# The conditioning row's products on GpSimd and their sums on ScalarE, where one VectorE operation did both

## Chip, cores and metric

The kernel runs as one program on one core of a Trainium2 chip. The metric is the device time of one execution in microseconds (us), lower is better; the time before is 2505.53 us, the median of three runs (2505.07 to 2505.62).

## What is computed

Two transformer blocks over 256 tokens of 2048 features, all in float32. Block 1 has a gated delta rule, a block attention, a merge of both through an output projection, and a convolutional feed-forward layer. Block 2 has two layers, each with a sparse attention, a retention and an output projection; each layer is modulated by a conditioning row `c` (1 x 2048):

```python
c_act = jax.nn.silu(c)
for l in range(DEPTH_2):
    mod = c_act @ w_mod[l] + b_mod[l]            # 3 * 2048 outputs
    shift, scale, gate = jnp.split(mod, 3, axis=-1)
    h = rmsnorm(x, norm_gain[l]) * (1.0 + scale[:, None, :]) + shift[:, None, :]
    proj = h @ w_in[l]
    ...
    x = x + gate[:, None, :] * y
```

The change is about `c_act @ w_mod[l]` alone: a product of one row with a 2048 x 6144 matrix, per layer.

## The kernel before

**Large products.** Every weight matrix is cut into granules of 128 x 1024 numbers (some are narrower). `load_w` (line 208) loads one granule into a buffer `w` (four of them), has ScalarE round it to a high part `wh` (line 215, three buffers), and has VectorE subtract that from `w` to give a low part `wl` (line 216, four buffers). TensorE then makes three products per 128 x 128 tile: high by both parts of the tokens' tile, low by its high part. There are 867 granules. TensorE's order is the order of emission, written out in Python; the other engines' order is set by the tile scheduler, from the order of emission and its own idea of durations.

**The modulation as a background job.** `modulation` (line 987) is a generator. For each layer `l`, quarter `q` of the 2048 inputs and chunk `f` of 128 outputs it loads a tile `mw` of 128 outputs x 512 inputs (256 KB) and lets one VectorE operation multiply it by the conditioning row `mc` (copied to all partitions, after Silu) and sum along the row into one column; the operation starts from the column of the quarter before, so that sums go to and fro between `part` and `modT[l]`. That is 2 x 4 x 48 = 384 tiles. `mod_sums(3)` leaves the three newest loads for later, so that a load has time to land. There are four `mw` buffers (tag `sig`).

**Its pace.** `load_w` calls `pace` after every granule, and `pace` emits so many steps of each job per granule: for the modulation 0.75 in the mixers of block 1, 1.2 in the merge and the output projection of block 1, 0.35 in the feed-forward layer, 0.8 in block 2 (`RATE`, line 32). Where a pool of buffers ends, `mod_to` (line 1009) finishes what is loaded and moves on. `behind` (line 223) makes what a job emits come after the granule's load, cast and subtraction on their queues. So on VectorE's queue stand `wl` of a granule, then a product with the row; on SP's queue, which issues all loads in order, stand a `w`, then an `mw` that waits for its buffer, and behind it the next `w`.

**Where it is used.** Layer 0's modulation is needed by `gains(0)` (line 931) at the end of the feed-forward layer, layer 1's at the end of layer 0 of block 2.

**The places that the steps below touch.** The output projection of block 1 is the call of `outs` in `merge` (line 648); its `done` (line 643) adds the product to the residual stream `x` (line 644), sums squares (`acc`, line 358) and splits `x` into `v` (lines 318 and 319). The mixers' chains of small products are in `gdn` (line 695): TensorE, ScalarE (line 771) and VectorE (lines 746 and 782) take turns. GpSimd does nothing but the small powers of `pow` (line 328), 55 in all.

Of the kernel before, what the change touches and what calls it, by code (L numbers as in the profile page):

```python
# [14 lines left out]
P = 128  # L15
# [14 lines left out]
NRAW = 7                        # first chunks of block 1 on the tiles without 1/rms  # L30
PACE = 2.0                      # between the normalized tiles
RATE = (0.75, 1.2, 0.35, 0.8)   # modulation per granule: mixers, merge, ffn, block 2

# ---------------------------------------------------------------------------
# constants that depend on shapes alone


def _consts():
# [4 lines left out]
    cm = np.where(c <= u, 0.0, NEG).astype(f)          # [t, s]: key s may be read by query t  # L43
# [7 lines left out]
    mt = np.where(c >= u, 0.0, NEG)                     # [s, c]  # L51
# [21 lines left out]
    diff = c - u                                        # [s, t]: t - s  # L73
# [39 lines left out]
# ---------------------------------------------------------------------------  # L113
# [5 lines left out]
class Net:  # L119
    """The tensor engine runs in the order of emission. Chains of small products (the mixers' heads)  # L120
    are tasks: generators that yield the time until their next stage; their stages are emitted
    between the k tiles of the large products."""
# [26 lines left out]
    def finish(self, t):  # L149
        """emit what is left of a task (others go on in its waits)"""  # L150
        while not t.done:
            q = min(self.tasks, key=lambda u: (u.ready, u is not t))
            self.clk = max(self.clk, q.ready)
            self.step(q)

    def job(self, name, gen, rate):
        """small pieces of work, rate of them per granule of weights"""
        self.jobs[name] = [gen, rate, 0.0]
# [26 lines left out]
    # -- small helpers  # L185
# [22 lines left out]
    def load_w(self, src, n):  # L208
        """One granule of weights from DRAM, as hi + lo parts."""
# [12 lines left out]
    @contextlib.contextmanager  # L222
    def behind(self):
        """issue what follows after the latest granule"""
        with self.tc.issue_after(self.latest[0]), self.tc.issue_after(self.latest[1]), \
                self.tc.issue_after(self.latest[2]):
            yield

    def gemm_b(self, ps, grans, mov, start=True, stop=True, hold=False):
        """ps[f, t] += sum_k W[k, f] x[t, k]; grans: (dram ap [128, k * 128], k tile ids).  # L230
        hold: leave out the last k tile and return a function that emits it."""
# [16 lines left out]
    def outs(self, grans, mov, done, hold=2, mid=None):  # L248
        """chunks whose last k tile may be late: the first ones leave it out at first"""
# [15 lines left out]
    def chunk(self, w, mov):  # L265
        """w: dram ap [2, 128, 1024]"""
# [4 lines left out]
    def chunks3(self, w, mov):  # L271
        """three chunks, k tile by k tile (for moving tiles that are just being made); w: [8, 128, 768]"""
# [15 lines left out]
    def gemm_a(self, w, n, mov, prep=None):  # L288
        """two token tiles of x @ W[:, block]; w: dram ap [8, 128, 2n]"""
# [21 lines left out]
    def split(self, dst, src, scale=None, bias=None):  # L311
        """dst[:, 0] + dst[:, 1] = scale * src (+ bias), in two parts of 12 bits each."""
# [37 lines left out]
    # -- norms over the features of the residual stream  # L350
# [9 lines left out]
    def tok_sums(self, accs):  # L360
        """column sums of feature-major [128, T] tiles -> psum [128 tokens, 2 * len]"""
# [7 lines left out]
    def rows(self, col, n):  # L369
        """[128 tokens, n] columns (two per row) -> psum [128, n * 128] with each row on all partitions"""  # L370
# [21 lines left out]
    def side(self, which, width=T):  # L392
        """one of the two sets of 16 split [128, T] tiles"""
# [3 lines left out]
    def raw(self, dst, k, gcol, shift=None):  # L397
        """dst = x[k] times the gain, not yet normalized; with the shift as one more column"""
# [5 lines left out]
    def normalize(self, wait, accs, cols, hs, gcol, shift=None, out=None):  # L404
        """task: 1/rms of the residual stream, and its normalized, split tiles hs"""
# [17 lines left out]
    def trig(self, pool, pos, tabs, ptag):  # L423
        """cos and signed sin tables [128, T] of pos * inv; tabs: [128, 2] inverse frequency, sign"""
# [22 lines left out]
    def rotate(self, out, ps, cos, sin, half):  # L447
        """out = ps * cos + swap(ps) * sin on the first 2 * half partitions, a copy on the rest"""
# [12 lines left out]
    # ---------------------------------------------------------------------  # L461
# [26 lines left out]
    # ---------------------------------------------------------------------  # L488
# [15 lines left out]
    def mixers(self, bo, b1):  # L504
# [55 lines left out]
        def early():  # L560
            """a chunk on the tiles without 1/rms while the others are made"""
# [90 lines left out]
    def conv(self, dst, ps, tap, width, bias=None):  # L652
        """dst[:, t] = sum_j tap(j) * ps[:, t - (width - 1) + j] (+ bias)"""
# [9 lines left out]
    def gdn_gates(self, ps, r):  # L663
        """beta [128, h, tt], g [128, tt, h] and the decay exponents that go per key"""
# [30 lines left out]
    def gdn(self, h, kq, v, z):  # L695
# [6 lines left out]
        # per-token norms of k and q  # L702
# [11 lines left out]
        # decay between key s (partition) and query c: blocks (0,0), (0,1), (1,1)  # L714
# [11 lines left out]
        # S: K00 K01 Q00 Q01 K11 Q11, keys on partitions, scaled by beta / |k|^2  # L726
# [12 lines left out]
        # inverse of I + A per tile of 128 tokens, by doubling; DE[:, 0] the inverse, DE[:, 1] its transpose  # L739
# [17 lines left out]
        # values, tokens on partitions, times |k|  # L757
# [45 lines left out]
        # output norm; the query norm and 1/sqrt(128) go in as one factor per token  # L803
# [21 lines left out]
    def softmax_pv(self, pool, S, mx, scale, vcols, out):  # L825
        """S [128, 384]: logits of token tile 0 (128 keys), tile 1 (256 keys); mx [128, 2] their maxima.
        appends to out: pv [d, t] = sum_s v[s, d] softmax(scale * S)[t, s]"""
# [40 lines left out]
    # ---------------------------------------------------------------------  # L868
# [62 lines left out]
    def gains(self, l):  # L931
        """gains of the norms of block 2 with the modulation in them"""
# [9 lines left out]
    def bias_table(self, pool):  # L942
        """job: bias [128 t, 384] per head: tile 0 keys 0..127, tile 1 keys 0..255"""
# [12 lines left out]
        nr = pool.tile([P, 3 * P], F32, tag="leaf", name="nr", bufs=5)      # pos_s - pos_t  # L956
# [3 lines left out]
        bk = pool.tile([P, 3 * P], F32, tag="leaf", name="bk", bufs=5)      # bucket number  # L960
# [11 lines left out]
        def tree(h, l, i):  # L972
            """entry of the bucket among rows [i << (l + 1), (i + 1) << (l + 1)) of the table"""
# [13 lines left out]
    def modulation(self):  # L987
        """job: modT[l] [128, 48] = silu(c) @ w_mod[l] + b_mod[l], feature-major (shift, scale, gate)"""
        nc = self.nc
        part = self.per.tile([P, 48], F32, name="part")  # L990
        for l in range(2):
            for q in range(4):
                s = slice(q * 512, (q + 1) * 512)
                src, dst, pool = (part, self.modT[l], None) if q % 2 else (self.modT[l], part, None)
                for f in range(48):
# [7 lines left out]
                    self.mod_ahead.append((w, c, src[:, f:f + 1], dst[:, f:f + 1]))  # L1003
                    self.mod_sums(3)
                    yield
            self.mod_sums(0)
            self.mod_done = l + 1

    def mod_to(self, pool, rate):
        """go on with the modulation in another pool"""  # L1010
        self.mod_sums(0)
        self.pmo = pool
        self.jobs["mod"][1:] = [rate, 0.0]

    def mod_sums(self, left):
        while len(self.mod_ahead) > left:
            w, c, src, dst = self.mod_ahead.pop(0)
            self.nc.vector.tensor_tensor_reduce(w, w, c, 1.0, src, OP.mult, OP.add, dst)  # L1018

    # ---------------------------------------------------------------------  # L1020
# [11 lines left out]
    def prepare(self, row):  # L1032
        """job: the residual stream of block 2 itself, and tables of the retention"""
# [11 lines left out]
    def layer(self, l):  # L1045
# [50 lines left out]
        # keys of the attention, with both gains and 1/rms in them  # L1096
        ka = b2.tile([P, T], F32, tag="ka", name="ka", bufs=1)
        key = self.add(self.keys(l, nxt(), ka))
        # queries
# [293 lines left out]
```

## Time and profile before

| | |
|---|---|
| median of three runs | 2505.53 us (2505.07 to 2505.62) |
| span of the profiled execution | 2502.3 us, first to last instruction |
| TensorE busy | 2486.1 us, 99% of the span |
| VectorE busy | 1931.8 us, 77% |
| ScalarE busy | 1400.8 us, 56% |
| GpSimd busy | 44.9 us, 2% |
| granted TensorE clock | 1.000 of full speed (2.4 GHz) |

The profiled execution's own time is not given beside its span; the runs' median is 3.2 us above the span, which is what lies before the first instruction and after the last. In the rows below, PE is TensorE, PEld its weight loads, DVE VectorE, ACT ScalarE, POOL GpSimd and SP the queue that issues the loads. A row of a wait names who waited, who released it, and the time in all. A matmul's end is modelled, so a busy TensorE is not one at its peak.

### The profile page before, as it was taken

What the parts mean: (1) busy time and instruction counts of PE and PEld (TensorE: products, weight loads), DVE (VectorE), ACT (ScalarE), POOL (GpSimd) and SP (SyncE); (2) the same over time, 40 slices, a digit from 0 to 9 for tenths busy, and PEclk for the clock granted to TensorE, in tenths of its full rate; (3) what the DMA queues carried; (4) which work ended last, traced back from release to release, by engine and by line L of the source; (5) the groups of instructions that cost most, each with busy time, mean ns of one, the idle gap of its engine ahead of it and who ended that gap; (6) DMA issues with size and microseconds to landing.
All of it is one profiled execution on the core that took longest, in us unless ns stands there. A gap on an engine that the chain in (4) does not pass through costs nothing.

```text
span 2502.3 us, 51550 instructions
## 1 busy us (share of the span) xinstructions
PE 2486.1 (99%) x20410; PEld 2474.0 (99%) x20410; DVE 1931.8 (77%) x3737; ACT 1400.8 (56%) x2240; POOL 44.9 (2%) x59
## 2 busy tenths in 40 slices
PE   8999999999999999999999999999999999999999
PEld 8999999999999999999999999999999999999999
DVE  8777778577799989889876679897887677666664
ACT  7555556534455656777754456655844456475443
POOL 0000000000000000000000000000000000000000
PEclk9999999999999999999999999999999999999999
DMA  6444476588889667767666767668676554444554
GB/s 240 169 154 161 149 228 226 200 281 304 297 286 306 211 215 213 237 218 218 234 219 213 238 216 218 210 216 275 212 239 220 180 185 167 157 169 167 176 185 159
DMA packets 189012, 536.06 MB, mean 214 GB/s; under 512 B 21600, under 2 KB 26464, under 8 KB 188768
## 3 DMA queue, kind: packets, MB, share of 16 engines
q1 hardware_dynamic: 188768, 532.75, 64.1%
q8 instruction: 160, 2.62, 0.4%
q14 instruction: 84, 0.69, 0.1%
HBM read 530.57 MB, written 2.10 MB: 213 GB/s over the span
## 4 chain that ended last, share of the span: by engine, by line
PE 96%; DVE 2%; ACT 1%; issue 0%; POOL 0%; DMA 0%; SPq 0%; DVEq 0%; POOLq 0%
PE mm L179 89%; PE aux L179 6%; PE aux L183 1%; DVE wl L216 0%; DVE isc L1228 0%; DMA w<-wA 0%; DVE mw L1018 0%; ACT wh L215 0%; DVE m L1232 0%; DVE isc L1233 0%; POOL rq L328 0%; DVE acc L358 0%; ACT L724 0%; ACT v L318 0%; POOL gf L328 0%
## 5 line engine op out<-in xcount | busy, mean ns | idle before, releaser
L179 PE MATMUL mm<-u,wh 128*128 128x256 f32 (+1 forms) x7488 | 1366.8, 284 | 0.0
L215 ACT CAST wh<-w 128x1024 fp32r<-128x1024 f32 (+5 forms) x867 | 854.1, 986 | 906.9 <-PE mm L179 752.6
L216 DVE TENSOR_TENSOR wl<-w,wh 128x1024 fp32r<-128x1024 f32 (+5 forms) x867 | 990.8, 1144 | 393.2 <-ACT wh L215 389.1
L179 PEld LDWEIGHTS mm<-u,wh 128*128 128x128 f32 x7488 | 1150.1, 189 | 3.9 <-issue 2.9
L179 PE MATMUL mm<-u,wl 128*128 128x256 f32 (+1 forms) x3744 | 1052.1, 281 | 0.0
L179 PE MATMUL mm<-v,wh 128*128 128x256 f32 (+1 forms) x4096 | 742.6, 283 | 0.0
L179 PEld LDWEIGHTS mm<-u,wl 128*128 128x128 f32 x3744 | 705.3, 188 | 0.0
L179 PEld LDWEIGHTS mm<-v,wh 128*128 128x128 f32 x4096 | 629.1, 189 | 0.8 <-issue 0.5
L179 PE MATMUL mm<-v,wl 128*128 128x256 f32 (+1 forms) x2048 | 576.4, 281 | 2.2 <-DVE wl L216 2.2
L179 PEld LDWEIGHTS mm<-v,wl 128*128 128x128 f32 x2048 | 385.8, 188 | 3.4 <-DVE wl L216 3.3
L1018 DVE CUSTOM_DVE_ANT_0 mw<-mw,mc,part 128x512 f32<-128x512 f32 x192 | 141.6, 744 | 4.3 <-ACT mc L1000 3.2
L1018 DVE CUSTOM_DVE_ANT_0 mw<-mw,mc,mod 128x512 f32<-128x512 f32 x192 | 142.2, 745 | 2.6 <-ACT mc L1000 2.5
L179 PE MATMUL mm<-wh,u 128*128 128x412 f32 (+1 forms) x320 | 88.9, 346 | 0.0
L976 ACT ACTIVATE leaf<-bit,row,dr 128x384 f32<-128x384 f32 x120 | 78.8, 698 | 0.0
L660 DVE SCALAR_TENSOR_TENSOR u<-mm,par,u 128x255 f32<-128x255 f32 (+1 forms) x160 | 76.3, 477 | 2.8 <-ACT u L658 2.1
L179 PE MATMUL mm<-wh,v 128*128 128x412 f32 (+1 forms) x256 | 69.8, 350 | 5.6 <-ACT wh L215 5.6
L179 PE MATMUL mm<-more,wh 128*128 128x256 f32 x384 | 69.7, 281 | 0.0
L179 PEld LDWEIGHTS mm<-wh,u 128*128 128x128 f32 x320 | 59.0, 188 | 0.4 <-issue 0.2
L179 PEld LDWEIGHTS mm<-more,wh 128*128 128x128 f32 x384 | 59.0, 189 | 0.0
L980 DVE COPY_PREDICATED leaf<-bit,leaf 128x384 f32<-128x384 uint32 x88 | 53.3, 605 | 3.4 <-ACT leaf L976 2.8
L179 PEld LDWEIGHTS mm<-wh,v 128*128 128x128 f32 x256 | 48.2, 192 | 6.7 <-ACT wh L215 6.6
L179 PE MATMUL mm<-wl,u 128*128 128x412 f32 (+1 forms) x160 | 54.2, 338 | 0.0
(293 smaller groups left out, 2014.5 us busy)
## 6 DMA issues: line engine op xcount, KB each, us to landing
w<-wB SPq DMA_DIRECT2D x344, 512.0 KB, 3.8
mw<-wM SPq DMA_DIRECT2D x384, 256.0 KB, 3.8
w<-wUp SPq DMA_DIRECT2D x170, 512.0 KB, 4.1
w<-wO SPq DMA_DIRECT2D x96, 512.0 KB, 4.3
w<-wDn SPq DMA_DIRECT2D x64, 384.0 KB, 3.5
w<-wDn SPq DMA_DIRECT2D x64, 320.0 KB, 3.4
w<-wA SPq DMA_DIRECT2D x48, 412.0 KB, 3.2
w<-wBr SPq DMA_DIRECT2D x32, 512.0 KB, 4.2
```

Of the source, the lines that this page charges most:

```text
L179: self.nc.tensor.matmul(out, l, r, start=start, stop=stop)
L183: self.nc.tensor.transpose(out, in_, self.c0("ident"))
L215: i1 = nc.scalar.copy(h[:, :n], w[:, :n])
L216: i2 = nc.vector.tensor_tensor(l[:, :n], w[:, :n], h[:, :n].bitcast(F32), op=OP.subtract)
L660: nc.vector.scalar_tensor_tensor(dst[:, s:], ps[:, :T - s], tap(width - 1 - s), dst[:, s:], op0=OP.mult, op1=OP.add)
L976: nc.scalar.activation(t, bits[0], ACT.Identity, scale=dr[:, i, h:h + 1], bias=rb[:, i, 0, h:h + 1])
L980: nc.vector.copy_predicated(t, bits[l].bitcast(mybir.dt.uint32), u)
L1018: self.nc.vector.tensor_tensor_reduce(w, w, c, 1.0, src, OP.mult, OP.add, dst)
```

## The change

Each tile `mw` is multiplied by the row in place by GpSimd, and a copy in place by ScalarE sums it along the row into a column of its own (`accum_out`). The columns of the four quarters no longer pass through one another: `part` has one per layer, quarter and chunk, and four small VectorE additions per layer put them together with the bias. The product is emitted two loads after its own, the sum three loads after, where the one VectorE operation stood. The scratch for dynamic DMA descriptors is made smaller (1024), and comments are left out; nothing else differs.

```diff
     def modulation(self):
...
-        part = self.per.tile([P, 48], F32, name="part")
+        part = self.per.tile([P, 2, 4, 48], F32, name="part")
         for l in range(2):
             for q in range(4):
                 s = slice(q * 512, (q + 1) * 512)
-                src, dst, pool = (part, self.modT[l], None) if q % 2 else (self.modT[l], part, None)
+                pool = None
                 for f in range(48):
...
                     w = pool.tile([P, 512], F32, tag="sig", name="mw", bufs=4)
                     nc.sync.dma_start(w, self.a["wM"][l, q, f])
-                    self.mod_ahead.append((w, c, src[:, f:f + 1], dst[:, f:f + 1]))
-                    self.mod_sums(3)
+                    self.mod_ahead.append([w, c, part[:, l, q, f:f + 1]])
+                    self.mod_sums(2, 3)
                     yield
-            self.mod_sums(0)
+            self.mod_sums()
+            for q in range(4):
+                nc.vector.tensor_tensor(self.modT[l], self.modT[l], part[:, l, q], op=OP.add)
             self.mod_done = l + 1
...
-    def mod_sums(self, left):
+    def mod_sums(self, loading=0, left=0):
+        nc = self.nc
+        for m in self.mod_ahead[:max(0, len(self.mod_ahead) - loading)]:
+            if m[1] is not None:
+                nc.gpsimd.tensor_tensor(m[0], m[0], m[1], op=OP.mult)
+                m[1] = None
         while len(self.mod_ahead) > left:
-            w, c, src, dst = self.mod_ahead.pop(0)
-            self.nc.vector.tensor_tensor_reduce(w, w, c, 1.0, src, OP.mult, OP.add, dst)
+            w, _, col = self.mod_ahead.pop(0)
+            nc.scalar.activation(w, w, ACT.Copy, accum_out=col)
...
-    nc = bacc.Bacc("TRN2", target_bir_lowering=False, num_devices=1)
+    nc = bacc.Bacc("TRN2", target_bir_lowering=False, num_devices=1, dynamic_dma_scratch_size=1024)
```

In the changed code the product stands in line 1022, the sum in line 1026 and the additions in line 1008. TensorE's instructions and their order are the same in both.

VectorE's queue before, in the output projection of block 1 (`x` is the residual stream, `acc` the sum of squares, `v` its split; L1018 is the product with the row, whose second row, with one column, reads the sum out):

```order
L216 TENSOR_TENSOR wl<-w,wh 128x1024
L1018 ISA mw,mod<-mw,mc,part 128x512
L1018 ISA mod 128x1
L644 TENSOR_TENSOR x_72<-x_72,mm 128x256
L216 TENSOR_TENSOR wl<-w,wh 128x1024
L358 TENSOR_TENSOR acc<-acc,sq 128x256
L319 SCALAR_TENSOR_TENSOR v_9102<-x_72,par,v_9102 128x256
L1018 ISA mw,mod<-mw,mc,part 128x512
L1018 ISA mod 128x1
L216 TENSOR_TENSOR wl<-w,wh 128x1024
```

The same place now:

```order
L216 TENSOR_TENSOR wl<-w,wh 128x1024
L644 TENSOR_TENSOR x_72<-x_72,mm 128x256
L216 TENSOR_TENSOR wl<-w,wh 128x1024
L358 TENSOR_TENSOR acc<-acc,sq 128x256
L319 SCALAR_TENSOR_TENSOR v_9267<-x_72,par,v_9267 128x256
L216 TENSOR_TENSOR wl<-w,wh 128x1024 x2
```

The products are gone from VectorE's queue, and the subtractions stand closer together.

ScalarE's queue before, in the same projection, a few granules later:

```order
L215 CAST wh<-w 128x1024 x2
L357 ACTIVATE sq<-x_73 128x256
L318 ACTIVATE v_9106<-x_73,par 128x256
L215 CAST wh<-w 128x1024 x2
L357 ACTIVATE sq<-x_73 128x256
```

And now, at the end of layer 0's modulation (`part` takes the sums):

```order
L215 CAST wh<-w 128x1024
L357 ACTIVATE sq<-x_73 128x256
L318 ACTIVATE v_9272<-x_73,par 128x256
L1026 ACTIVATE mw,part<-mw 128x512
L215 CAST wh<-w 128x1024
L1026 ACTIVATE mw,part<-mw 128x512
L215 CAST wh<-w 128x1024
L357 ACTIVATE sq<-x_74 128x256
L318 ACTIVATE v_9273<-x_74,par 128x256
L1026 ACTIVATE mw,part<-mw 128x512 x4
L215 CAST wh<-w 128x1024
```

A sum, which waits for GpSimd's product, stands between the casts, and four in a row where the layer's last loads are finished.

GpSimd's queue now, from the mixers to the feed-forward layer (`gcp`, `gf` and `rc` are the powers of norms, which stood next to one another before):

```order
L328 TENSOR_TENSOR gcp<-gcs,cst_79 128x4
L1022 TENSOR_TENSOR mw<-mw,mc 128x512 x5
L328 TENSOR_TENSOR gf<-gso,cst_79 128x2
L1022 TENSOR_TENSOR mw<-mw,mc 128x512 x10
L328 TENSOR_TENSOR gf<-gso,cst_79 128x2
L1022 TENSOR_TENSOR mw<-mw,mc 128x512 x151
L328 TENSOR_TENSOR rc<-rc,cst_79 128x2
```

The powers now stand behind the products, one to ten of them apart in the mixers.

## Rows read from the trace of the kernel before

**Rows 1.** The page's busy time, share of the span and instructions of each engine.

```profile
PE 2486.1 (99%) x20410; PEld 2474.0 (99%) x20410; DVE 1931.8 (77%) x3737; ACT 1400.8 (56%) x2240; POOL 44.9 (2%) x59
```

**Rows 2.** TensorE's waits: who released it, us in total, times, longest.

```profile
PE mm L179 <- ACT wh L215: 5.6, 3, 4.6
PE mm L179 <- DVE wl L216: 3.7, 7, 1.1
PE aux L179 <- ACT gR L771: 2.6, 2, 2.0
```

**Rows 3.** Busy us by stretch: from:to and length, PE, PEld, DVE, ACT, POOL, clock, DMA.

```profile
0.00:100.00 100.00, 91.05 (x688) 87.07 (x689) 79.16 (x165) 73.16 (x134) 3.96 (x7) 1.00 0.63 218
100.00:200.00 100.00, 96.36 (x808) 94.51 (x808) 72.39 (x150) 51.10 (x105) 4.47 (x5) 1.00 0.46 154
```

**Rows 4.** The same for merge (first) and output projection of block 1 (second).

```profile
500.00:690.00 190.00, 190.00 (x1604) 190.00 (x1604) 147.78 (x259) 77.66 (x91) 0.00 (x0) 1.00 0.86 295
690.00:820.00 130.00, 130.00 (x1098) 130.00 (x1098) 117.84 (x235) 65.42 (x98) 0.00 (x0) 1.00 0.85 288
```

**Rows 5.** The same two stretches, VectorE's operations on the tile mw alone.

```profile
500.00:690.00 190.00, 57.82 (x79) 1.00 0.86 295
690.00:820.00 130.00, 40.10 (x55) 1.00 0.85 288
```

**Rows 6.** VectorE's groups by form: busy us, mean ns, idle before and its releaser.

```profile
L216 DVE TENSOR_TENSOR wl<-w,wh 128x1024 fp32r<-128x1024 f32 x642 | 784.8, 1223 | 319.9 <-ACT wh L215 317.6
L1018 DVE CUSTOM_DVE_ANT_0 mw<-mw,mc,mod 128x512 f32<-128x512 f32 x192 | 142.2, 745 | 2.6 <-ACT mc L1000 2.5
L1018 DVE CUSTOM_DVE_ANT_0 mw<-mw,mc,part 128x512 f32<-128x512 f32 x192 | 141.6, 744 | 4.3 <-ACT mc L1000 3.2 <-DMA mw<-wM 1.1
...
L216 DVE TENSOR_TENSOR wl<-w,wh 128x640 fp32r<-128x640 f32 x64 | 52.5, 820 | 16.7 <-ACT wh L215 16.5
```

**Rows 7.** ScalarE's groups by form, and the casts of the projection's stretch (last).

```profile
L1000 ACT ACTIVATE mc<-mc 128x512 f32<-128x512 f32 x11 | 6.9, 628 | 10.9 <-DMA mc<-c 10.9
...
L833 ACT ACTIVATION_READ_ACCUMULATOR aS<-aS,snm 128x1 f32 x32 | 6.0, 187 | 0.0
...
L215 ACT CAST wh<-w 128x1024 fp32r<-128x1024 f32 x43 | 45.1, 1050 | 53.3 <-PE mm L179 44.1 <-issue 7.0 <-ACT v L318 2.0
```

**Rows 8.** GpSimd's groups: busy us, mean ns, idle before.

```profile
L328 POOL TENSOR_TENSOR brs<-bve,cst 128x2 f32<-128x2 f32 x16 | 11.1, 696 | 474.2 <-DVE bve L1280 474.2
L328 POOL TENSOR_TENSOR gcp<-gcs,cst 128x4 f32<-128x4 f32 x8 | 8.2, 1027 | 125.6 <-DVE gcs L708 125.6
```

**Rows 9.** Timeline: start us, us, engine; a power alone, and one beside VectorE.

```profile
1653.98 0.69 POOL L328 TENSOR_TENSOR rq<-hr,cst 128x2 f32<-128x2 f32 x1 [5.16 <-DVE hr L1185]
...
1703.15 1.00 DVE L216 TENSOR_TENSOR wl<-w,wh 128x824 fp32r<-128x824 f32 x1
...
1703.31 1.40 POOL L328 TENSOR_TENSOR rq<-hr,cst 128x2 f32<-128x2 f32 x1 [3.94 <-DVE hr L1185]
```

**Rows 10.** VectorE's groups by form in the stretch 690 to 820 us.

```profile
L216 DVE TENSOR_TENSOR wl<-w,wh 128x1024 fp32r<-128x1024 f32 x43 | 52.4, 1220 | 10.0 <-ACT wh L215 9.8
...
L319 DVE SCALAR_TENSOR_TENSOR v<-x,par,v 128x256 fp32r<-128x256 f32 x16 | 7.6, 477 | 0.0
...
L358 DVE TENSOR_TENSOR acc<-acc,sq 128x256 f32<-128x256 f32 x15 | 6.3, 417 | 0.0
L319 DVE SCALAR_TENSOR_TENSOR u<-mrg,u 128x256 fp32r<-128x256 f32 x16 | 6.0, 416 | 0.0
...
L216 DVE TENSOR_TENSOR wl<-w,wh 128x768 fp32r<-128x768 f32 x3 | 2.8, 950 | 0.4 <-ACT wh L215 0.4
L634 DVE TENSOR_TENSOR mrg<-sig 128x256 f32<-128x256 f32 x5 | 2.1, 419 | 0.1
```

**Rows 11.** All waits: ScalarE's casts for a buffer that TensorE gives back.

```profile
ACT wh L215 <- PE mm L179: 752.6, 553, 4.2
```

**Rows 12.** The page's loads: times, KB each, median us from issue to landing.

```profile
mw<-wM SPq DMA_DIRECT2D x384, 256.0 KB, 3.8
```

More of the change, by code (lines that the diff above doesn't have):

```diff
@@ L1002, in modulation @@
                     nc.sync.dma_start(w, self.a["wM"][l, q, f])
-                    self.mod_ahead.append((w, c, src[:, f:f + 1], dst[:, f:f + 1]))
-                    self.mod_sums(3)
+                    self.mod_ahead.append([w, c, part[:, l, q, f:f + 1]])
+                    self.mod_sums(2, 3)
                     yield
-            self.mod_sums(0)
+            self.mod_sums()
+            for q in range(4):
+                nc.vector.tensor_tensor(self.modT[l], self.modT[l], part[:, l, q], op=OP.add)
             self.mod_done = l + 1
     def mod_to(self, pool, rate):
-        self.mod_sums(0)
+        self.mod_sums()
         self.pmo = pool
         self.jobs["mod"][1:] = [rate, 0.0]
-    def mod_sums(self, left):
+    def mod_sums(self, loading=0, left=0):
[4 more added lines that the diff above has]
+                m[1] = None
         while len(self.mod_ahead) > left:
-            w, c, src, dst = self.mod_ahead.pop(0)
-            self.nc.vector.tensor_tensor_reduce(w, w, c, 1.0, src, OP.mult, OP.add, dst)
+            w, _, col = self.mod_ahead.pop(0)
+            nc.scalar.activation(w, w, ACT.Copy, accum_out=col)
     def block2(self, b2):
```

## The prediction, made blind

> **What bounds the kernel now.** I read the busy times first, then TensorE's waits, then the busy time stretch by stretch. TensorE is busy for 2486.1 of 2502.3 us, 99%, and its instructions are the same after the change [rows 1]. So 16.2 us is all that the profile shows as idle, and the waits put it down to few places: the casts and subtractions of the first granules, and a chain in the mixers that waits for ScalarE's copy `gR`, 2.6 us in two waits [rows 2]. By stretch, 8.95 us of the idle time lie in the first 100 us and 3.64 us in the second [rows 3]; in the merge and in the output projection of block 1 TensorE never stops [rows 4]. VectorE (77%) and ScalarE (56%) run ahead of it: ScalarE's casts wait 752.6 us for a buffer that TensorE has to give back, in 553 waits [rows 11]. That is how a reader sees who sets the pace: the helper waits for the bound engine, not the other way.
>
> The job begins after the first heads, so of the idle time it could reach only the mixers' 3.6 us and scraps. A measurement of this kernel can tell about 0.2%, 5.0 us, from no change. More than that can't be gained, whatever VectorE is spared; the question is whether TensorE begins to wait.
>
> **The change, part by part.** The median of the runs, 2505.5 us, is 3.2 us above the span; I add my terms to the median, since nothing in the change touches what lies outside the span.
>
> *VectorE loses* 384 operations of 0.745 us, 283.8 us busy [rows 6], and gains eight additions of 48 columns. In the projection it is busy for 117.8 of 130 us [rows 4], of which the products are 40.1 [rows 5]. All of it is hidden under TensorE today: 0 us gained.
>
> *ScalarE gains* 384 copies of 128 x 512 with a sum. A Silu of that size takes 0.628 us and reading out a sum 0.187 us [rows 7]: at most 0.82 us each, 313 us in all, and ScalarE goes to about 1714 us, 68%. In the merge that makes 77.7 + 79 x 0.82 = 142 of 190 us, in the projection 65.4 + 55 x 0.82 = 110 of 130 us [rows 4, 5]. The cover is the casts' waiting for TensorE, 44.1 us of the projection [rows 7], and 45 us are wanted there: just enough, if no sum waits. Cost 0.
>
> *GpSimd gains* 384 products of 128 x 512, which no row shows. From below: VectorE's own pass, 0.745 us [rows 6]. From above: a power of two columns takes 0.696 us and one of four 1.027 [rows 8], 0.166 us per column, which for 512 columns would be 85 us a product and 33 ms in all. A power is another computation, and the row that the product is nearest to is a plain subtraction: from 640 to 1024 columns it grows from 820 to 1223 ns, 1.05 ns per column [rows 6]. I take GpSimd's 0.70 us of two columns as what every instruction costs and add 512 columns at that rate, 0.54 us: 1.23 us. If the two operands are read one after the other, it is 0.70 + 1.08 = 1.78 us, the upper end that I keep. GpSimd is then busy for some 517 us, 21%.
>
> For the same product the Trainium skill, GPSIMD Engine Reference, section "Performance versus the Vector engine", gives 4497 ns for 2048 columns, and calls it about twice VectorE's time; my estimate from that page for 512 columns is a quarter, 1.12 us, and the sum below would stand. No run here shows it.
>
> *The wait that is added.* A sum now waits for a product, and the product for its load; behind the sum on ScalarE's queue stand the next cast, and for that cast wait VectorE's subtraction and TensorE. The freed `mw` buffer lets SP issue the next load, and behind that stand the weights. Four buffers and 79 products in 190 us [rows 5] make a turn of 4 x 2.41 = 9.6 us. Landing 3.8 us [rows 12], product 1.23 and sum 0.82 make 5.9 us: 3.8 us are left, and with 1.78 us still 3.2. In the projection the turn is 4 x 2.36 = 9.5 us. Cost 0.
>
> *The five places where loads are finished at once* (three ends of pools, two ends of layers) leave no such room: the last sum follows its load at once, and what comes on top is one product, 1.23 us. The casts are one to two granules ahead (46 granules in 130 us are 2.8 us each [rows 4, 10]), so I let a quarter through: 5 x 0.3 = 1.5 us. From below 0, from above 5 x 1.78 = 9 us.
>
> *The mixers.* VectorE's share gets lighter, ScalarE's copies get a neighbour, and GpSimd's powers stand behind products. Between losing the 3.6 us of idle time and adding as much again I take 0.
>
> *GpSimd beside VectorE.* The timeline shows that GpSimd can be made to wait: a power that takes 0.69 us alone takes 1.40 us when it starts beside a subtraction, and ends 0.56 us after that subtraction does (1704.71 against 1704.15) [rows 9]. The other direction, VectorE waiting for a long GpSimd product, no row can show, since a power reads two columns. I bound it. If it never happens: 0. If every product stops VectorE for its whole 1.23 us: in the merge 79 x 1.23 = 97 us, against 42.2 us that VectorE is idle and 57.8 us that it is spared, 100 in all: it fits. In the projection 55 x 1.23 = 67.7 us, against 12.2 + 40.1 = 52.3 us: 15.4 us too much. But a product meets VectorE only when the next operation has two operands in SBUF, if it is as beside the subtraction, which has two [rows 9]. Those are the subtractions, `v`, `acc`, `u` and `mrg` [rows 10]: 52.4 + 2.8 + 7.6 + 6.3 + 6.0 + 2.1 = 77.2 of 130 us, 59%. 0.59 x 67.7 = 40 us, less than 52.3. I take 0, and keep 15.4.
>
> Sum: 2505.5 + 1.5 = **2507 us**.
>
> **The rivals.**
>
> *GpSimd's products hold up VectorE in the output projection of block 1* (the call in line 648). Then the subtractions come late, one after another, until TensorE has used up what is done ahead. The price is worked out above: 15.4 us, less one granule of 2.8 us that is ahead at its start, plus the 1.5: 2505.5 + 14 = 2520 us. It decides from 52.3 / 55 = 0.95 us that a product costs VectorE on average. For it speaks that GpSimd waits to the end of a subtraction, so something is shared [rows 9], and that VectorE has only 12.2 us to spare there [rows 4]. Against it speaks the 59%. Chance 0.25.
>
> The Trainium skill, SBUF — State Buffer, section "Who interferes with whom", states this as a rule against the change: a VectorE instruction with two SBUF inputs and a GpSimd instruction that reads SBUF share a read port, and whichever comes second is blocked until the first is done. The trace agrees with one half of it, 1.40 against 0.69 us [rows 9]; if both halves hold fully the time is this rival's.
>
> *Lateness on the short chains.* `gcp` and `gf` are sixteen powers in the mixers on which later stages wait, and each may find half a product before it: 16 x 0.62 = 10 us if nothing hid it. ScalarE's sums may delay the `gR` copies, whose two waits cost 1.3 us each today [rows 2]. TensorE has rows of large products between the stages, so I let two thirds through: 2505.5 + 6.6 = 2512 us. Chance 0.09.
>
> *A gain.* With VectorE lighter the mixers' idle 3.6 us [rows 3] go: 2505.5 - 3.6 = 2502 us. It would need more than all of it to be told from no change. Chance 0.03.
>
> That the change doesn't do what it says is no rival: the queues shown above have the products on GpSimd and the sums on ScalarE.
>
> **How the numbers follow.** The forecast has 0.63, the rivals 0.25, 0.09 and 0.03. Slower by over 5 us are the first two rivals: 0.34. Faster by over 5 us: 0.03. Within: 0.63. The range must leave out no more than 2 in 10: it goes down to 2503, short of the full gain, and up to 2520, the first rival's price; products of 1.78 us would cost more (55 x 1.78 = 98 us against 52.3), and with part of the gain are what I leave out. The forecast's own range is 2503 to 2510.
>
> **What would show it.** Right: TensorE busy again for some 2486 us, and its waits for `wl` and `wh` still a few us; VectorE at 1650 to 1750 us; ScalarE near 1700; GpSimd near 520, with products of 1.1 to 1.4 us; the casts still waiting for TensorE, less than 752.6 us. Wrong: subtractions of 128 x 1024 whose mean has grown well over 1.22 us, and TensorE idle between 690 and 820 us waiting for `wl` (first rival); waits of TensorE's small products on ScalarE or GpSimd between 100 and 470 us (second); products of 1.8 us or more, with ScalarE's sums waiting for GpSimd and casts late behind them.

## Result and the profile after

The changed kernel takes **2546.4 us** (median of four runs, 2543.99 to 2550.18) against 2505.6 us before, measured beside it: ratio 1.0164, 95% interval 1.015 to 1.0178. It is 41 us slower. The forecast was 2507 us, and the range ended at 2520.

First the page's busy times after the change, the answer to [rows 1]:

```profile
PE 2503.6 (98%) x20410; PEld 2483.2 (98%) x20410; DVE 1906.6 (75%) x2977; ACT 1628.3 (64%) x3008; POOL 650.5 (26%) x443
```

Two numbers were not foreseen. VectorE lost 283.8 us of products [rows 6] and is busy only 25.2 us less: what it has left takes 1906.6 - (1931.8 - 283.8) = 258.6 us longer, 0.67 us per product of GpSimd. And TensorE, with the same instructions, is idle for 2542.2 - 2503.6 = 38.6 us in place of 16.2, and "busy" for 17.5 us more.

TensorE's waits, the answer to [rows 2] (who waited, who released it, us in all, times, longest):

```profile
PE mm L179 <- DVE wl L216: 16.9, 24, 1.9
PE aux L179 <- ACT gR L771: 7.0, 4, 3.1
PE mm L179 <- ACT wh L215: 6.8, 4, 4.6
```

VectorE's low parts `wl` are late 24 times in place of 7, for 16.9 us in place of 3.7; the mixers' `gR` 4 times in place of 2. Next VectorE's groups by form, the answer to [rows 6] (busy us, mean ns of one, idle before and its releaser):

```profile
L216 DVE TENSOR_TENSOR wl<-w,wh 128x1024 fp32r<-128x1024 f32 x642 | 854.9, 1333 | 343.7 <-ACT wh L215 341.3 <-issue 0.3
...
L216 DVE TENSOR_TENSOR wl<-w,wh 128x640 fp32r<-128x640 f32 x64 | 58.7, 917 | 18.8 <-ACT wh L215 18.5
```

The same subtractions take 1333 ns in the mean in place of 1223, and 917 in place of 820. The output projection of block 1 now runs from 707 to 846 us. Its groups answer to [rows 10]:

```profile
L216 DVE TENSOR_TENSOR wl<-w,wh 128x1024 fp32r<-128x1024 f32 x43 | 72.4, 1686 | 9.8 <-ACT wh L215 9.7
L319 DVE SCALAR_TENSOR_TENSOR v<-x,par,v 128x256 fp32r<-128x256 f32 x15 | 15.5, 1032 | 0.0
L319 DVE SCALAR_TENSOR_TENSOR u<-mrg,u 128x256 fp32r<-128x256 f32 x16 | 13.8, 895 | 0.0
L358 DVE TENSOR_TENSOR acc<-acc,sq 128x256 f32<-128x256 f32 x14 | 13.5, 963 | 0.0
L644 DVE TENSOR_TENSOR x<-x,mm 128x256 f32<-128x256 f32 x16 | 6.5, 409 | 0.4 <-PE mm L179 0.4
```

Four groups have grown: `wl` from 1220 to 1686 ns, `v` from 477 to 1032, `u` from 416 to 895, `acc` from 417 to 963. The fifth has not: `x<-x,mm` reads one operand from PSUM (`mm` is TensorE's result), and takes 409 ns; it was 416. In this stretch all groups that have grown read two operands in SBUF. For comparison GpSimd's product, ScalarE's sum and its read-out, over the whole execution:

```profile
L1022 POOL TENSOR_TENSOR mw<-mw,mc 128x512 f32<-128x512 f32 x384 | 606.5, 1588 | 1173.9 <-DMA mw<-wM 849.3
```

```profile
L1026 ACT ACTIVATE mw<-mw 128x512 f32<-128x512 f32 x384 | 240.4, 626 | 16.7 <-POOL mw L1022 16.1
...
L1026 ACT ACTIVATION_READ_ACCUMULATOR mw<-mw 128x1 f32 x384 | 72.5, 189 | 0.0
```

The timeline shows single pieces (start us, us, engine). First VectorE, then GpSimd, in the projection, and then in the mixers:

```profile
770.40 0.41 DVE L644 TENSOR_TENSOR x<-x,mm 128x256 f32<-128x256 f32 x1
770.73 1.99 DVE L216 TENSOR_TENSOR wl<-w,wh 128x1024 fp32r<-128x1024 f32 x1
772.64 1.51 DVE L358 TENSOR_TENSOR acc<-acc,sq 128x256 f32<-128x256 f32 x1
774.08 1.52 DVE L319 SCALAR_TENSOR_TENSOR v<-x,par,v 128x256 fp32r<-128x256 f32 x1
775.52 1.21 DVE L216 TENSOR_TENSOR wl<-w,wh 128x1024 fp32r<-128x1024 f32 x1
```

```profile
765.67 9.64 POOL L1022 TENSOR_TENSOR mw<-mw,mc 128x512 f32<-128x512 f32 x5
```

```profile
226.97 1.23 DVE L813 SCALAR_TENSOR_TENSOR gf<-gf,gcp 128x2 f32<-128x2 f32 x1 [0.62 <-POOL gf L328]
```

```profile
226.91 1.28 POOL L1022 TENSOR_TENSOR mw<-mw,mc 128x512 f32<-128x512 f32 x1
```

While five products run one after another, from 765.67 to 775.31 us, every two-SBUF operation beside them is stretched; at 775.52, with GpSimd at rest, a subtraction takes 1.21 us again. In the mixers an operation of two columns starts 0.06 us after a product and lasts 1.23 us, until the product is over (226.91 + 1.28 = 228.19; 226.97 + 1.23 = 228.20). That is VectorE waiting out a product.

One operand in SBUF can be enough. `rq<-rq`, a product with a constant in block 2, has a median of 0.17 us in its 16 instances. Four of them start beside a product and last until it is over, as this one (first VectorE, then GpSimd):

```profile
1707.88 1.26 DVE L1188 TENSOR_SCALAR rq<-rq 128x2 f32<-128x2 f32 x1 [0.59 <-POOL rq L328]
```

```profile
1707.82 1.29 POOL L1022 TENSOR_TENSOR mw<-mw,mc 128x512 f32<-128x512 f32 x1
```

**Where the 41 us lie.** TensorE's order is unchanged, so each matmul can be set beside the same matmul of before, and the difference of their starts read at the ends of the stages (the matmul that started at 470.0 us starts at 482.6). In the profiled executions, 39.9 us apart: mixers 12.6, merge 4.1, output projection and what follows to 830 us 9.8, feed-forward layer 1.9, start of block 2 (to 1800 us before) 11.3, the rest 0.2. By the distance from one matmul to the next: 27.1 us are 30 places where it grew by over 0.3 us, 6.2 us lie in four stretches at the lower of the clock's two levels (1.2 GHz), and the remainder is small pieces. These four stretches are in the following windows (from:to, length, PE busy and count, clock, DMA share, GB/s):

```profile
193.00:202.00 9.00, 5.88 (x38) 0.81 0.39 138
355.00:363.00 8.00, 6.13 (x39) 0.79 0.66 233
686.00:694.00 8.00, 5.89 (x36) 0.79 0.95 342
805.00:814.00 9.00, 7.48 (x47) 0.81 0.82 270
```

Before each of them TensorE had stood for 1.0 to 3.4 us from one matmul's start to the next; before the change the mean granted clock was 1.000 over the whole execution. Not every such stand was followed by a lower clock: one of 2.2 us from 815.5 us was not.

### The profile page after: what moved, and what is told of

It reads as the page before. It is cut to its first block, busy times and chain, and to the rows that moved or that the text cites. A ratio compares the mean times of both kernels' runs of the same rounds, so it can differ in the third digit from the quotient of the medians.

```text
span 2542.2 us, 52289 instructions
## 1 busy us (share of the span) xinstructions
PE 2503.6 (98%) x20410; PEld 2483.2 (98%) x20410; DVE 1906.6 (75%) x2977; ACT 1628.3 (64%) x3008; POOL 650.5 (26%) x443
## 4 chain that ended last, share of the span: by engine, by line
PE 87%; DVE 5%; ACT 3%; issue 2%; DMA 2%; POOL 1%; SPq 0%; ACTq 0%; DVEq 0%; POOLq 0%
PE mm L179 81%; PE aux L179 6%; DVE wl L216 2%; ACT wh L215 1%; DMA mw<-wM 1%; DMA mc<-c 1%; POOL mw L1022 1%; PE aux L183 1%; ACT mw L1026 0%; DVE acc L358 0%; DVE v L319 0%; DMA w<-wA 0%; DVE u L319 0%; DVE u L1203 0%; ACT u L318 0%
## 5 line engine op out<-in xcount | busy, mean ns | idle before, releaser
L216 DVE TENSOR_TENSOR wl<-w,wh 128x1024 fp32r<-128x1024 f32 (+5 forms) x867 | 1079.5, 1247 | 416.5 <-ACT wh L215 412.6
L1022 POOL TENSOR_TENSOR mw<-mw,mc 128x512 f32<-128x512 f32 x384 | 606.5, 1588 | 1173.9 <-DMA mw<-wM 849.3
L1026 ACT ACTIVATE mw<-mw 128x512 f32<-128x512 f32 x384 | 240.4, 626 | 16.7 <-POOL mw L1022 16.1
L328 POOL TENSOR_TENSOR brs<-bve,cst 128x2 f32<-128x2 f32 x16 | 11.2, 698 | 275.4 <-DVE bve L1288 275.3
L980 DVE COPY_PREDICATED leaf<-bit,leaf 128x384 f32<-128x384 uint32 x88 | 67.6, 769 | 12.7 <-ACT leaf L976 11.9
L1026 ACT ACTIVATION_READ_ACCUMULATOR mw<-mw 128x1 f32 x384 | 72.5, 189 | 0.0
```

Of the source, the lines that this page charges most:

```text
L216: i2 = nc.vector.tensor_tensor(l[:, :n], w[:, :n], h[:, :n].bitcast(F32), op=OP.subtract)
L328: self.nc.gpsimd.tensor_tensor(out, in_, e, op=OP.pow)
L980: nc.vector.copy_predicated(t, bits[l].bitcast(mybir.dt.uint32), u)
L1022: nc.gpsimd.tensor_tensor(m[0], m[0], m[1], op=OP.mult)
L1026: nc.scalar.activation(w, w, ACT.Copy, accum_out=col)
```

## The experiments

**Is it ScalarE's sums or GpSimd's products?** The products go back to VectorE, the sums stay on ScalarE (`e1`); or the products stay on GpSimd, and VectorE makes the sums (`e2`).

```diff
-                nc.gpsimd.tensor_tensor(m[0], m[0], m[1], op=OP.mult)
+                nc.vector.tensor_tensor(m[0], m[0], m[1], op=OP.mult)      # e1
...
-            nc.scalar.activation(w, w, ACT.Copy, accum_out=col)
+            nc.vector.reduce_sum(col, w, axis=mybir.AxisListType.X)       # e2
```

> The change with one part undone: the products go back to VectorE (a plain multiply), the sums stay on ScalarE. GpSimd has only its 55 powers again. Theory A (a product on GpSimd and a VectorE operation with two operands in SBUF lock each other out, 1.29 us against 1.22 us, and that is what TensorE waits for): within 5 us of before, 2503 to 2511 us, subtractions of 128 x 1024 at 1.22 us mean again, no stretch of half clock between 690 and 820 us. Theory B (the sums on ScalarE, and the wait for a product that they bring into its queue, make the casts late): at least half of the 41 us stay, 2526 us or more, with TensorE waiting for wh and for the gR copies.

> The change with the other part undone: products on GpSimd, the sums on VectorE as a reduction with one operand in SBUF (some 0.69 us by the row of 128 x 512 operations), nothing added to ScalarE. Theory A: as slow as the change or slower, 2546 us or more, since the products still lock VectorE and VectorE has 384 x 0.69 = 265 us more to do; wl at 1.3 us mean or more. Theory B: clearly faster than the change, 2525 us or less. The part of the mixers (100 to 460 us), where the change lost 12.5 us: if it is ScalarE's sums that made the gR copies late, TensorE's wait for them falls from 7.0 us back to 2.6.

`e1` took 2507.28 us, ratio 1.0004 (0.9994 to 1.0013): the whole loss is gone with the products, and behind VectorE's products ScalarE's sums cost nothing. The rest of the change, the smaller DMA scratch too, is still in `e1`. `e2` took 2574.25 us, ratio 1.0271 (1.0256 to 1.0287): more than the change; VectorE, with the sums as well, is busy for 2083.5 us.

**Does a product cost time when nothing reads its result?** The kernel before, with a GpSimd product into a tile that nothing reads (`e3`; VectorE's operation writes to a tile of its own there), or a fill of the used tile, which writes and reads nothing (`e5`), or three such fills, as long as a product beside VectorE (`e13`).

```diff
+            self.nc.gpsimd.tensor_tensor(self.dg, w, c, op=OP.mult)       # e3
-            self.nc.vector.tensor_tensor_reduce(w, w, c, 1.0, src, OP.mult, OP.add, dst)
+            self.nc.vector.tensor_tensor_reduce(self.dv, w, c, 1.0, src, OP.mult, OP.add, dst)
...
+            self.nc.gpsimd.memset(w, 0.0)                                 # e5; e13: three times
```

> The kernel before, and beside each of its 384 VectorE operations a GpSimd product of the same tile and the row into a tile that nobody reads. No sum waits for a product; only the load buffer is given back a little later. VectorE writes its products to another tile instead of in place. Theory A: slower than the change, since VectorE keeps its 284 us and the lock comes on top: 2550 to 2600 us, with the loss in the merge and the output projection (500 to 820 us) above all, because VectorE is busy there for 78 to 91 of 100 us without it. Theory B: within 8 us of before, since nothing waits for a product.

> The kernel before, and behind each of its 384 VectorE operations a GpSimd fill of the tile with zeros, which writes SBUF and reads nothing; the next load into the buffer waits for it. Control for the extra products: the same queue, places and waits of the powers, but no reading. If it is GpSimd's reading that locks VectorE: 2503 to 2511 us, subtractions at 1.22 us. If any GpSimd work does it, or the powers behind it on GpSimd's queue: 2515 us or more.

> The kernel before, with three fills by GpSimd of each tile behind VectorE's product: GpSimd is busy for as long as in the changed kernel (3 x 0.53 = 1.6 us a tile, about 650 us in all), and its powers stand behind that work, but it reads no SBUF. Theory A, that only a product's reading blocks VectorE: 2504 to 2511 us, subtractions of 128 x 1024 at 1.22 to 1.23 us. Rival B, that the mixers' loss comes from powers that stand behind long work on GpSimd: about 2515 to 2525 us, with the loss between 100 and 470 us.

`e3`: 2661.73 us, ratio 1.0614 (1.0597 to 1.0632), more than expected. `e5`: 2506.47 us, 1.0004 (0.9995 to 1.0013). `e13`: 2506.15 us, 1.0003 (0.9993 to 1.0012). The busy times, of `e3` and of `e13`:

```profile
PE 2540.5 (96%) x20410; PEld 2503.0 (94%) x20410; DVE 2227.9 (84%) x3737; ACT 1397.1 (53%) x2240; POOL 679.4 (26%) x443
```

```profile
PE 2487.4 (99%) x20410; PEld 2475.9 (99%) x20410; DVE 1938.4 (77%) x3737; ACT 1401.1 (56%) x2240; POOL 647.6 (26%) x1211
```

GpSimd is as busy in both, 679 and 648 us. Where it reads SBUF, VectorE's time grows by 2227.9 - 1931.8 = 296 us, 0.77 us per product, with work whose result nobody reads; only the next load into the buffer waits for it, as it does for the fills. Where GpSimd only writes, VectorE's grows by 6.6 us. `e13` also settles the powers that stand behind other work on GpSimd's queue: between 100 and 470 us it loses 2.0 us (read as above), against the change's 12.6.

**Does one operand lock as two do, and does length count?** As `e3`, with a copy in place of the product (`e14`), or a product of 256 columns (`e18`).

```diff
-            self.nc.gpsimd.tensor_tensor(self.dg, w, c, op=OP.mult)
+            self.nc.gpsimd.tensor_copy(self.dg, w)                        # e14
+            self.nc.gpsimd.tensor_tensor(self.dg[:, :256], w[:, :256], c[:, :256], op=OP.mult)  # e18
```

> The kernel before, with a copy by GpSimd of each tile into a tile that nothing reads, where the run with extra products had a product: one SBUF operand is read in place of two. Theory A1, that any reading of SBUF by GpSimd blocks VectorE's operations with two SBUF operands: clearly slower than before, 2540 to 2662 us, with subtractions well over 1.23 us. Theory A2, that only a GpSimd instruction with two SBUF operands does: 2504 to 2511 us and subtractions of 1.22 to 1.23 us.

> The kernel before, with a product of 256 of the 512 columns by GpSimd into a tile that nothing reads. Alone it should take 0.73 us, close to the copy's 0.62, but read two SBUF operands where the copy reads one. Theory L, that what is lost goes by the time that GpSimd reads: near the copies' run, 2518 to 2535 us. Theory T, that a product with two SBUF operands blocks VectorE more than a copy of like length: half of the whole products' loss or more, 2570 to 2620 us.

`e14`: 2520.22 us, ratio 1.0059 (1.0044 to 1.0074). `e18`: 2540.66 us, 1.013 (1.0115 to 1.0145). Both lie outside what either of their theories gave: a copy does block, so two operands are not needed, but far less than a product. GpSimd's groups, of `e14`, then of `e18`:

```profile
L1020 POOL COPY dg<-mw 128x512 f32<-128x512 f32 x384 | 364.4, 949 | 1410.8 <-DMA mw<-wM 1409.3
```

```profile
L1020 POOL TENSOR_TENSOR dg<-mw,mc 128x256 f32<-128x256 f32 x384 | 395.6, 1030 | 1400.7 <-DMA mw<-wM 1131.2 <-ACT mc L1002 265.4
```

The shortest of them, which ran alone, take 0.61 and 0.73 us, a whole product 1.26. VectorE's busy time grows by 73.5, 119.3 and (`e3`) 296.1 us; the kernel by about 14, 34 and 156 us. The loss rises much faster than the blocked time: the first of it fits into VectorE's idle time, the last of it does not. Whether a second operand counts apart from length these runs don't separate.

**Does the loss go by the number of products or by place?** Every fourth product on GpSimd, the others on VectorE (`e9`, sums on ScalarE); each product in two instructions of 256 columns (`e12`).

```diff
-                nc.gpsimd.tensor_tensor(m[0], m[0], m[1], op=OP.mult)
+                self.nmod = getattr(self, 'nmod', 0) + 1                  # e9
+                (nc.vector if self.nmod % 4 else nc.gpsimd).tensor_tensor(m[0], m[0], m[1], op=OP.mult)
...
+                for j in range(2):                                        # e12
+                    z = slice(256 * j, 256 * j + 256)
+                    nc.gpsimd.tensor_tensor(m[0][:, z], m[0][:, z], m[1][:, z], op=OP.mult)
```

> The change with every fourth product on GpSimd and three of four on VectorE: 96 locks in place of 384. If the loss goes by the number of locks: a quarter of 41 us, 2513 to 2518 us. If it needs VectorE to be out of spare time for whole stretches (it has some again when only a quarter locks): within 4 us of the change without GpSimd, 2505 to 2511 us.

> The change with each product made in two GpSimd instructions of 256 columns: shorter locks, twice as many, and more GpSimd time in all (each starts anew). If what counts is how long one lock lasts (a late subtraction or a late link of a chain): faster than the change, 2525 to 2540 us. If it is the time locked in all: the same or slower, 2546 us or more.

`e9`: 2518.2 us, ratio 1.0048 (1.0034 to 1.0061), 12 us, somewhat over a quarter of the loss for a quarter of the products. By stage it lies in the mixers, 6.7 us, and at the start of block 2, 6.1, while merge and projection lose under 1. I read this so that in the two last VectorE makes up for one blocked operation in four; why the two first lose more than a quarter no run shows. `e12`: 2541.64 us, 1.0134 (1.0118 to 1.015), between what its theories gave; it touches the change's interval and tells nothing.

**Can the job move out of the mixers?** The rate of the job in the mixers set to 0 and in the feed-forward layer to 0.6, in the kernel before (`e8`) and in the changed one (`e10`).

```diff
-RATE = (0.75, 1.2, 0.35, 0.8)
+RATE = (0, 1.2, 0.6, 0.8)
```

> The kernel before with another pace: no modulation in the mixers, 0.6 instead of 0.35 per granule in the feed-forward layer. VectorE does all as before. If VectorE's operations with the row are what makes the mixers' chains late today, up to 4 us faster, 2502 to 2504 us; if the feed-forward layer, where VectorE is busy for 90 of 100 us, has no room for them, 2506 us or more. A candidate for a better kernel.

> The change with the pace of the run before last in this list (none in the mixers, 0.6 in the feed-forward layer), so 73 or so products move from the mixers to a stretch where TensorE has no chains to wait for. The mixers' 12.5 us should go, 2532 to 2536 us, if they come from products locking VectorE in the chains' gaps; if the feed-forward layer has too little room at 0.6, what is saved comes back there, 2540 us or more.

`e8`: 2507.03 us, 1.0003 (0.9994 to 1.0012). `e10`: 2546.19 us, 1.016 (1.0146 to 1.0174). By stage `e10` loses nothing more in the mixers (-1.3 us), but 12.2 us in the feed-forward layer in place of 1.9 and 18.3 at the start of block 2 in place of 11.3. The loss follows the products.

**Do reloads of the row hold up the weights?** The row `mc` has one buffer, and its next quarter is loaded through SP's queue when the last product has read it. SP's queue at 672 us of before, then at 676 us after the change:

```profile
671.50 0.33 SPq L212 DMA_DIRECT2D w<-wBr  x1
672.17 0.33 SPq L999 DMA_DIRECT2D mc<-c  x1
672.55 0.42 SPq L1002 DMA_DIRECT2D mw<-wM  x1
674.35 0.33 SPq L212 DMA_DIRECT2D w<-wBr  x1
```

```profile
676.37 0.33 SPq L212 DMA_DIRECT2D w<-wB  x1
682.36 0.33 SPq L999 DMA_DIRECT2D mc<-c  x1
682.78 0.86 SPq L1002 DMA_DIRECT2D mw<-wM  x2
683.73 0.38 SPq L212 DMA_DIRECT2D w<-wB  x1
```

And GpSimd's last products of that quarter:

```profile
676.01 1.49 POOL L1022 TENSOR_TENSOR mw<-mw,mc 128x512 f32<-128x512 f32 x1 [0.75 <-DMA mw<-wM]
679.95 2.38 POOL L1022 TENSOR_TENSOR mw<-mw,mc 128x512 f32<-128x512 f32 x1 [2.46 <-ACT wh L215]
```

The last product ends at 682.33 us, and 0.03 us later the row's load goes out, with the weights behind it: SP issued nothing for 5.7 us. Two buffers for the row (`e16`):

```diff
-                        c = pool.tile([P, 512], F32, tag="mc", name="mc", bufs=1)
+                        c = pool.tile([P, 512], F32, tag="mc", name="mc", bufs=2)
```

> The changed kernel with two buffers for the conditioning row in place of one. In the changed kernel the reload of the row at the end of a quarter waits for the quarter's last product: four times SP's queue, with the weights behind it, issues nothing for 3.1, 3.8, 5.7 and 5.5 us (at 349, 566, 682 and 805 us), where before the longest such gap was 0.9 us. Theory A alone, that all of the loss comes from VectorE's blocked operations: 2543 to 2549 us. Theory C, that part of it comes from these reloads: 2532 to 2539 us, with the merge and the projection giving most of what is won, and the mixers and block 2 as slow as now.

`e16`: 2538.46 us, ratio 1.0125 (1.0108 to 1.0142), 8 us less than the change, whose interval begins at 1.015, and as theory C had it in size. By stage the merge loses 0.0 us in place of 4.1; the projection still 9.4, which theory C had not, so the reloads' share there was small. The two profiled executions are only 4.6 us apart, so of the 8 us the traces place 4.1 in the merge and little elsewhere.

**Do blocked operations reach TensorE directly, or through late sums on ScalarE?** Both with two buffers for the row: each product one load earlier (`e19`), and no sums at all (`e20`, which so leaves the modulation uncomputed).

```diff
-                    self.mod_sums(2, 3)
+                    self.mod_sums(1, 3)                                   # e19
...
+        nc.vector.memset(part, 0.0)                                       # e20
-            nc.scalar.activation(w, w, ACT.Copy, accum_out=col)
```

> The changed kernel with two buffers for the row, and each product emitted one load after its own in place of two, so that a sum has more room behind its product. Theory A, that VectorE's blocked operations cost what is left of the loss: as with two rows, 2534 to 2544 us. Theory S, that ScalarE's sums wait for products that come late, and the casts behind them: 2512 to 2530 us.

> The changed kernel with two buffers for the row and without the sums: ScalarE does nothing for the modulation, VectorE makes no products, and GpSimd's products only hold up VectorE. The sums are left out, so the modulation's outputs are not computed. Theory A, that VectorE's blocked operations cost it: 2530 to 2540 us. Theory S, that the casts standing behind late sums cost it: 2504 to 2515 us. In between the loss is shared.

`e19`: 2536.29 us, 1.0125 (1.0108 to 1.0141). `e20`: 2533.02 us, 1.0118 (1.0103 to 1.0133). Both times lie in theory A's range. The busy times and TensorE's longest waits of `e20`:

```profile
PE 2498.3 (99%) x20410; PEld 2480.4 (98%) x20410; DVE 1908.0 (75%) x2978; ACT 1399.3 (55%) x2240; POOL 649.5 (26%) x443
```

```profile
PE mm L179 <- DVE wl L216: 14.6, 19, 1.9
```

ScalarE makes no sums here, VectorE no products, and still TensorE waits for `wl` nearly as long as in the changed kernel (14.6 us against 16.9), and the kernel loses 1.2%. GpSimd's products alone are enough for a loss of this size.

By stage, though, it is not the loss of `e16`, which is the same kernel with the sums: 6.3 us in the mixers in place of 13.1, 3.1 in the projection in place of 9.4, and 15.8 at the start of block 2 in place of 10.5. In the projection `wl` is as long as there (1688 ns in the mean against 1614), and yet TensorE loses a third as much. So it is partly chance that the totals agree, and theory S is not excluded for the mixers and the projection: sums that wait for products may have had a share there. Why block 2 loses more stays open.

No version beat the kernel before; `e1`, `e5`, `e8` and `e13` equal it.

## Why the prediction was wrong, by its steps

**The step that failed** is the last term, "GpSimd beside VectorE": "0.59 x 67.7 = 40 us, less than 52.3. I take 0, and keep 15.4." In its place the runs showed most of the 41 us: the loss goes with the products (`e1`), and work of the same length on GpSimd that reads nothing does not bring it (`e13`); up to 8 us come another way, by the reloads below (`e16`). The term's size was right. In the projection the lengthened groups add 43 x 0.466 = 20.0 us (`wl`), 15 x 0.555 = 8.3 (`v`), 16 x 0.479 = 7.7 (`u`) and 14 x 0.546 = 7.6 (`acc`): 43.6 us, beside the 40 that I had worked out. What was wrong was the zero. I compared a sum with a sum and called what fits hidden. VectorE's work comes in a row, though: `wl`, `acc`, `v` and `wl` again, with five products beside them, and there it falls behind by up to about a microsecond per operation. In the merge and the projection (from:to, length, PE, PEld, DVE, ACT, POOL):

```profile
509.00:707.00 198.00, 195.89 (x1637) 195.48 (x1636) 129.49 (x103) 128.10 (x253) 134.41 (x81) 0.99 0.85 287
707.00:846.00 139.00, 133.53 (x1092) 131.50 (x1091) 125.56 (x127) 96.46 (x205) 89.26 (x53) 0.99 0.79 266
```

VectorE is busy for 125.56 of 139 us, 90%, and so it was before [rows 4]: the products that left are replaced by waiting. TensorE, which never stopped here, is idle for 5.5 us in the projection, nearly all of it by waits for `wl`:

```profile
PE mm L179 <- DVE wl L216: 4.7, 6, 1.9
```

**The first rival's mechanism was right, and its place too narrow.** It put the whole loss in the projection, 14 us; the projection with what follows gave 9.8. Another 23.9 us are in the mixers and at the start of block 2, where I had written "I take 0" for the mixers and nothing for block 2. TensorE waits for different things in these two places. First its waits in the mixers (100 to 483 us; three smaller ones left out), then at the start of block 2 (1555 to 1820 us):

```profile
PE aux L179 <- ACT gR L771: 7.0, 4, 3.1
PE aux L183 <- ACT gsq L816: 1.6, 1, 1.6
PE mm L179 <- DVE wl L216: 1.2, 2, 0.7
```

```profile
PE mm L179 <- DVE wl L216: 6.6, 9, 1.4
PE aux L179 <- ACT sq L1185: 0.6, 1, 0.6
PE aux L179 <- ACT spt L843: 0.3, 1, 0.3
```

In the mixers the chains of small products come late, 8.6 us of waits for `gR` and `gsq` in place of 3.6. The small operations of a chain are blocked like large ones there, `gf<-gf,gcp` of two columns for 1.23 us, as the timeline shows, and TensorE's next small product waits for the chain's end. VectorE's idle share, on which I had weighed everything, says nothing about a chain. At the start of block 2 it is late subtractions, as in the projection: 6.6 us of waits for `wl` in place of 0.3 (1530 to 1800 us of before).

The Trainium skill, SBUF — State Buffer, section "Who interferes with whom", has the rule that the second comer of the two engines is blocked until the first is done. The trace now agrees with both halves: a product that takes 1.28 us alone took 2.38 beside VectorE, and an `acc` of 0.42 us took 1.51 beside products. I gave it 0.25, by the mean share of 59%; weighed operation by operation it would have had more.

**The step on the places where loads are finished** was wrong in what it counted. It priced five ends of pools and layers at 0.3 us each. Quarters end too, and there SP's queue waited for the last product before it reloaded the row: four gaps of 3.1 to 5.7 us, 8 us of the result by `e16`. The prediction counted what stands behind the `mw` loads on SP's queue and left out the `mc` loads on the same queue.

**The second rival**, powers behind products and `gR` behind sums, was wrong in its first half: powers behind fills cost the mixers 2.0 us (`e13`). Its second half stays open. ScalarE's sums cost nothing behind VectorE's products (`e1`), but behind GpSimd's products the waits for `gR` grew from 2.6 to 7.0 us. With two rows they are 5.6 us (`e16`), without the sums 3.2 (`e20`), with the sums on VectorE 6.3 (`e2`): the blocked chain and sums that stand before `gR` can both have a part in it.

**What was right.** The product's own size, 1.23 us forecast and 1.26 to 1.30 alone, since it ends up at 1.59 in the mean only by waiting. ScalarE's 0.82 us (626 + 189 ns) and the cover of its casts: they still wait for TensorE, less than in [rows 11]:

```profile
ACT wh L215 <- PE mm L179: 534.0, 463, 3.4
```

VectorE's spared time brought nothing, as said. Off were GpSimd's 517 us, which became 650.5 with the powers, and VectorE's 1650 to 1750 us, which became 1906.6, both by the lock. The subtractions' mean "well over 1.22 us" and TensorE's waits for `wl` in the projection were the signs that the prediction had named for its first rival.

The clock is a loss of its own, 6.2 us, which no step had: each time it fell, TensorE had been made to stand shortly before.

**Left open:** how much of the loss in the mixers and the projection goes by sums that wait for products; and what of the 17.5 us by which TensorE is "busy" for longer is waiting that its modelled ends hide (the lower clock explains 6.2).

## What to carry to other kernels

Work given to GpSimd is not free because GpSimd is idle: if it reads SBUF, look at VectorE's operations beside it, above all those with two operands in SBUF, and count every product as that much of VectorE's time (here 0.67 to 0.77 us per product of 512 columns, nearly the 0.745 us that VectorE itself had needed). Whether it fits is not a question of sums over a stretch: look at the rows that VectorE has to get through one after another, and at the short chains, where an operation of two columns can wait as long as one of 1024. And where a slower engine now reads a buffer last, look for every load that reuses the buffer, and for what stands behind that load on its queue.

## What the runs showed that was not expected

- Fills by GpSimd, 1.6 us per tile in `e13`, left VectorE's subtractions at 1224 ns and the kernel at 1.0003: writing did not block here, reading did.
- A GpSimd copy of 512 columns, one operand read, takes 0.61 us alone, half of a product's 1.26; a product of 256 columns takes 0.73.
- The loss is far from proportional to the blocked time: 73.5 us blocked cost 14 us, 119.3 cost 34, 296.1 cost 156 (`e14`, `e18`, `e3`).
